# One layer-one planner step: the turn of an output behind more products, and new start times for the threads of the last two head pairs

## The chip, the cores and the metric

The kernel runs on one core of a Trainium2 chip. What counts is the time of one execution on the device, in microseconds (us). Times inside an execution are read from a hardware profile and count from the start of its span.

## What is computed

A trunk of two layers on 1024 tokens of width 1024: a gated linear recurrence (HGRN2) with 16 heads of 128, then forgetting attention (FoX). The change lies in the first layer:

```python
q, fz, i, g = jnp.split(h @ w_in, 4, axis=-1)
logf = jnp.log(lb + (1.0 - lb) * jax.nn.sigmoid(fz))
k = (1.0 - lb) * jax.nn.sigmoid(-fz)
b = jnp.cumsum(logf, axis=3)                       # in chunks of 64 tokens
q_dec, k_in, k_st = q * jnp.exp(b), k * jnp.exp(-b), k * jnp.exp(b_last - b)
att = jnp.where(causal, jnp.einsum('bhnck,bhnsk->bhncs', q_dec, k_in), 0.0)
o_intra = jnp.einsum('bhncs,bhnsv->bhncv', att, v)
...
    o = jnp.einsum('bhck,bhkv->bhcv', qd, state)
    state = dl[..., None] * state + jnp.einsum('bhck,bhcv->bhkv', ks, vv)
...
o = _rms(o, onorm_g.reshape(A_HEADS, HEAD_DIM)).reshape(bsz, s, WIDTH)
return (o * jax.nn.silu(g)) @ w_out
```

## The kernel before

**Two kinds of work.** Layer one multiplies h with 32 weight matrices of 256 columns: for each of eight head pairs p one for v, f, q and g. From the second half of the list on, each is done in seven *steps* (`sa_step`, lines 733 to 760) by a Strassen-like scheme, a step being 12 *products* (matmuls of 128 x 512). A step's weights are made ready two steps ahead (`sa_prep`): GpSimd forms sums (lines 727 to 731), ScalarE rounds (line 242), GpSimd or VectorE subtracts (line 243). The finished columns go to DRAM (lines 644, 647, 758, 759). Beside that VectorE sums modulation weights for later (`mod_sum`, lines 280 and 283, one line 280 and seven lines 283 for each of 24 matrices).

The recurrence of a pair is done by four *threads* (p, i), i = 0 to 3: head j = i % 2, token half th = i // 2. Here they are counted 0 to 31 over all pairs. A thread (`hg_thread`) does:

- *load* (line 494): forget rows f, then q and v, from DRAM into the blocks of its head;
- *forget* (`hg_forget`, lines 495 to 525): ScalarE's sigmoids (502, 503) and logarithm (506), VectorE's scan (507), small steps (513 to 517), ScalarE's exponentials (518 to 521), VectorE's products (522 to 525), GpSimd's line 508;
- *attention* (`hg_att`): 16 small matmuls, the mask (538), four transposes of the keys; *values* (`hg_values`): four transposes;
- *state* (`hg_state`) and *output* (`hg_out`): matmuls, ScalarE's square (580), VectorE's sum (582), the root in twelve small steps (`rsqrt_mean`, lines 231 to 237), and the scaling (584);
- *turn* (`hg_turn`): four transposes of line 584's result on TensorE, ScalarE's line 596, GpSimd's 597, four stores (599).

The blocks of a head are used again by the thread two places on: its load waits for the store of the turn, since f lands where the turn's result lies. Line numbers of matmuls and transposes are those of the recording helpers (48 and 51).

**What sets the order.** The class `Weave` records TensorE's instructions in the order in which they are to run. Products are written out in a plain loop, and each tells the planner by `tick` how much planned time went by; threads are generators that `yield` the planned time until their next part, and a part is put in as soon as it is due. `wait` holds a thread until a mark is set. The recorded order of TensorE is binding. The order of the other engines is made by a scheduler from dependencies and from the program's order, so it moves with TensorE's. `hg_spawn` gives the four threads of a pair their planned start times. Each engine takes its instructions in order; SyncE issues all transfers.

After the list of matrices the output projection of layer one begins (`out_proj`); its first products still alternate with the last threads, 28 to 31.

Of the kernel before, what the change touches and what calls it, by code (L numbers as in the profile page):

```python
# [20 lines left out]
NP = H // 2  # L21
# [72 lines left out]
def hybrid_trunk_kernel(ctx: ExitStack, tc: tile.TileContext, x, c, mod_w, mod_b, norm_g, a_w_in,  # L94
# [4 lines left out]
    PE = Weave(tc, nc.tensor)  # L99
# [391 lines left out]
    def hg_load(p, i):  # L491
        u = us[i % 2]
        for kind, n in (("f", "lf"), ("q", "qd"), ("v", "v")):
            dma(u[n], hgd[kind, p, i])

    def hg_forget(p, i, before):


        j = i % 2
        h, u = 2 * p + j, us[j]  # L500
        oc, lc = oml[:, h:h + 1], lb[:, h:h + 1]
        S.activation(u["k"], u["lf"], AF.Sigmoid, scale=-1.0)
        S.activation(u["lf"], u["lf"], AF.Sigmoid)
        if before is not None:
            S.activation(us[before]["ks"], us[before]["g"], AF.Sigmoid)
        S.activation(u["lf"], u["lf"], AF.Ln, bias=lc, scale=oc)
        V.tensor_tensor_scan(u["b"], rst, u["lf"], 0.0, ALU.mult, ALU.add)  # L507
        G.tensor_scalar(u["k"], u["k"], oc, 0.0, ALU.mult, ALU.add)
        b, k, lf, ks, kst = [ab(u[n]) for n in ("b", "k", "lf", "ks", "kst")]

        dl = sml.tile([P, 8], F32, tag=f"dl{j}", name="dl")
        col = dl.rearrange("p (n o) -> p n o", o=1)
        V.tensor_copy(col[:, 0:4], b[:, :, 0, 63:64])
        V.tensor_copy(col[:, 7:8], b[:, 3:4, 1, 63:64])
        V.tensor_tensor(col[:, 4:7], b[:, 0:3, 1, 63:64], b[:, 1:4, 0, 63:64], ALU.add)
        V.tensor_tensor(lf[:, :, 1, :], spread(dl[:, 4:8], 4, 64), b[:, :, 1, :], ALU.subtract)  # L516
        V.tensor_tensor(b[:, :, 0, :], b[:, :, 0, :], spread(dl[:, 0:4], 4, 64), ALU.subtract)
        S.activation(dl, dl, AF.Exp)
        S.activation(u["ks"], u["b"], AF.Exp, scale=-1.0)
        S.activation(u["eb"], u["b"], AF.Exp)  # L520
        S.activation(lf[:, :, 1, :], lf[:, :, 1, :], AF.Exp)  # L521
        V.tensor_tensor(u["qd"], u["qd"], u["eb"], ALU.mult)  # L522
        V.tensor_tensor(u["ks"], u["ks"], u["k"], ALU.mult)
        V.tensor_tensor(kst[:, :, 1, :], k[:, :, 1, :], lf[:, :, 1, :], ALU.mult)
        V.tensor_tensor(kst[:, :, 0, :], ks[:, :, 0, :], spread(dl[:, 4:8], 4, 64), ALU.mult)
        u["dl"] = dl

    def hg_att(j):

        u = us[j]  # L530
        pa, pk = c128(sm_ps()), sm_ps()
        ks, qd, kst = c128(u["ks"]), c128(u["qd"]), c128(u["kst"])
        for n in range(4):
            PE.matmul(pa[0:64, n, :], lhsT=ks[:, n, 0:64], rhs=qd[:, n, :], start=True, stop=True)
            PE.matmul(pa[64:P, n, 64:P], lhsT=ks[:, n, 64:P], rhs=qd[:, n, 64:P], start=True, stop=True)
        for rows, cs in ((slice(0, 64), slice(0, P)), (slice(64, P), slice(64, P))):
            m = keep[rows, cs]
            V.copy_predicated(u["att"][rows, :, cs],  # L538
                              m.rearrange("p (o q) -> p o q", o=1).broadcast_to([64, 4, m.shape[1]]), pa[rows, :, cs])
        for n in range(4):  # L540
            PE.transpose(pk[:, n * P:(n + 1) * P], kst[:, n, :], ident)
        S.activation(u["kT"], pk, AF.Copy)

    def hg_values(j):

        v, pv = us[j]["v"], sm_ps()
        for n in range(4):
            PE.transpose(pv[:, n * P:(n + 1) * P], v[:, n * P:(n + 1) * P], ident)
        S.activation(v, pv, AF.Copy)

    def hg_state(j, th):

        u = us[j]
        pu = sm_ps()
        kT, st, dl, v = c128(u["kT"]), c128(u["S"]), u["dl"], c128(u["v"])
        nl = 3 if th == 1 else 4
        for n in range(nl):
            PE.matmul(pu[:, n * P:(n + 1) * P], lhsT=kT[:, n, :], rhs=v[:, n, :], start=True, stop=True)
        with tc.high_priority():
            if th == 1:  # L560
                V.tensor_scalar(st[:, 0, :], st[:, 0, :], dl[:, 0:1], None, ALU.mult)
            for n in range(nl):
                if th == 0 and n == 0:
                    V.tensor_copy(st[:, 1, :], pu[:, 0:P])
                else:
                    V.scalar_tensor_tensor(st[:, (n + 1) % 4, :], st[:, n, :], dl[:, 4 + n:5 + n],
                                           pu[:, n * P:(n + 1) * P], ALU.mult, ALU.add)

    def hg_out(j, th):
        u = us[j]  # L570
        po = oa_ps()
        pov = c128(po)
        att, qd, st, v = u["att"], c128(u["qd"]), c128(u["S"]), c128(u["v"])
        for n in range(4):
            first = th == 0 and n == 0
            PE.matmul(pov[:, n, :], lhsT=att[:, n, :], rhs=v[:, n, :], start=True, stop=first)
            if not first:
                PE.matmul(pov[:, n, :], lhsT=qd[:, n, :], rhs=st[:, n, :], start=False, stop=True)
        sq = u["sq"]
        S.activation(sq, po, AF.Square)  # L580
        ss = sml.tile([P, 4], F32, name="ss")
        V.tensor_reduce(ss, c128(sq), AX.X, ALU.add)
        r = rsqrt_mean(ss, 4, 1.0 / P)
        V.tensor_tensor(c128(sq), pov, spread(r, 4, P), ALU.mult)  # L584

    def hg_turn(p, i):

        j, th = i % 2, i // 2
        h, u = 2 * p + j, us[j]
        if (p, i) == (NP - 1, 3):  # L590
            S.activation(u["ks"], u["g"], AF.Sigmoid)
        G.tensor_tensor(u["g"], u["g"], u["ks"], ALU.mult)
        pg = sm_ps()
        for n in range(4):
            PE.transpose(pg[:, n * P:(n + 1) * P], u["sq"][:, n * P:(n + 1) * P], ident)
        S.activation(u["ogT"], pg, AF.Copy, scale=ongc[:, h:h + 1])  # L596
        G.tensor_tensor(u["ogT"], u["ogT"], u["g"], ALU.mult)  # L597
        for n in range(4):
            dma(ogd[th * 4 + n][:, h, :], u["ogT"][:, n * P:(n + 1) * P])

    def hg_thread(p, i):

        j, th = i % 2, i // 2
        first, last = (p, i) == (0, 0), (p, i) == (NP - 1, 3)
        before = (p, i - 1) if i else (p - 1, 3)
        if i >= 2 or p > 0:
            yield from PE.wait(("turn", *((p, i - 2) if i >= 2 else (p - 1, i + 2))))
        for kind in "fqv":
            yield from PE.wait(("mat", kind, p, i))
        hg_load(p, i)  # L610
        yield 3.5
        if not first:
            yield from PE.wait(("gate", *before))
        hg_forget(p, i, None if first else 1 - j)
        PE.marks.add(("forget", p, i))
        yield 9.5
        hg_att(j)
        yield 2.5
        hg_values(j)
        yield from PE.wait(("mat", "g", p, i))  # L620
        dma(us[j]["g"], hgd["g", p, i])
        PE.marks.add(("gate", p, i))
        yield 2.0
        hg_state(j, th)
        yield 4.0
        hg_out(j, th)
        yield 9.0 if p < NP - 2 else 8.0
        if not last:
            yield from PE.wait(("forget", *((p, i + 1) if i < 3 else (p + 1, 0))))
        hg_turn(p, i)  # L630
        PE.marks.add(("turn", p, i))
        yield 0.0
# [65 lines left out]

    def hg_spawn(p):
        for i in range(4):  # L700
            PE.spawn(hg_thread(p, i), {NP - 2: (2.0, 19.0, 35.0, 51.0), NP - 1: (2.0, 14.0, 34.0, 46.0)}.get(
                p, (2.0, 21.0, 40.0, 59.0))[i])


# [59 lines left out]
    G.memset(rst, 1.0)  # L764
    G.memset(c64(rst)[:, :, 0:1], 0.0)
    hg_spawn(0)
    sa_prep(0)
    sa_prep(1)
# [4 lines left out]
    for i, (n, m) in enumerate(SSTEPS):  # L773
        if m == 3 and n + 2 < len(MATS):
            load(a_w(*MATS[n + 2]), 12 + n % 2)
        if m == 7 and n < len(mods_left):
            acc = accs[n % 2]
            mod_sum((18, acc))
            PE.spawn(mod_later(mods_left[n], acc), 8.0)
        if m == 4 and n + 1 < len(mods_left):  # L780
            load(mod_src(mods_left[n + 1]), 18)
        sa_prep(i + 2)
        sa_step(i)
        if m == 4 and MATS[n][0] == "q":
            hg_spawn(MATS[n][1])
# [739 lines left out]
```

## Time and profile before

| | |
|---|---|
| median of three runs | 2527.96 us (2522.85 to 2529.18) |
| the profiled execution | 2524.89 us, its span 2522.9 us |
| TensorE matmuls | 2251.0 us (89%) |
| TensorE weight loads, beside them | 1955.8 us (78%) |
| VectorE | 1717.2 us (68%) |
| ScalarE | 1117.5 us (44%) |
| GpSimd | 879.0 us (35%) |
| mean granted TensorE clock | 0.954 |

The engines are shown as PE (TensorE matmul), PEld (its weight loads), DVE (VectorE), ACT (ScalarE), POOL (GpSimd) and SP (SyncE). A timeline row is a run of like instructions: start, length, engine, line, operation, output and inputs, count, and in brackets the idle time before it with what ended it. The threads of the recurrence run from about 140 to 1170 us of the span.

### The profile page before, as it was taken

The numbers are of one execution on the slowest core, as the hardware profiler recorded it, in microseconds if no ns is written. First come the engines' busy times: TensorE is split into PE (matmuls) and PEld (weight loads), VectorE is DVE, ScalarE is ACT, GpSimd is POOL, SyncE is SP. The second block draws the span as 40 slices with busy tenths as digits, with TensorE's granted clock in tenths as the row PEclk, the third lists the DMA queues.
The fourth block names the chain that finished last, engine by engine and source line by source line (L and its number), as shares of the span: only waits on it lengthen the run. The fifth ranks groups of instructions, "written<-read, shape, count | busy, mean of one in ns | idle before, by whom it ended". The sixth has DMA issues, their size and how long they took to land.

```text
span 2522.9 us, 37602 instructions
## 1 busy us (share of the span) xinstructions
PE 2251.0 (89%) x13384; PEld 1955.8 (78%) x13384; DVE 1717.2 (68%) x4032; ACT 1117.5 (44%) x1850; POOL 879.0 (35%) x755
## 2 busy tenths in 40 slices
PE   4988877887777788889988899989999999999999
PEld 3766666666666677668878899989999999998887
DVE  7687777766676766675586864866777667767633
ACT  5434444444444455563333332444445444455421
POOL 3544444444444455410022222233333333332100
PEclk9999989988888999889999999999999999999999
DMA  7354434344443333474643232351222222325443
GB/s 242 114 163 138 146 119 136 122 137 130 134 137 122 126 113 118 127 246 141 188 137 96 78 118 84 101 167 59 72 78 85 80 86 61 94 74 159 162 144 117
DMA packets 257183, 312.28 MB, mean 124 GB/s; under 512 B 18706, under 2 KB 187060, under 8 KB 256996
## 3 DMA queue, kind: packets, MB, share of 16 engines
q1 hardware_dynamic: 256996, 309.88, 39.0%
q8 instruction: 106, 1.74, 0.3%
q14 instruction: 81, 0.66, 0.1%
HBM read 229.91 MB, written 79.90 MB: 123 GB/s over the span
## 4 chain that ended last, share of the span: by engine, by line
PE 59%; DVE 23%; issue 5%; ACT 3%; DMA 3%; POOL 1%; SPq 0%; DVEq 0%; ACTq 0%; POOLq 0%
PE mm L48 37%; PE oa L48 9%; PE sm L48 7%; PE sm L51 6%; DVE rows4k L283 4%; DVE blk L243 2%; DVE blk L507 1%; DVE rs_t L235 1%; ACT L521 1%; DVE rs_t L232 1%; DVE rs_t L236 1%; DVE rs_y L237 1%; DVE blk L584 1%; DVE blk L758 1%; DVE blk L522 1%
## 5 line engine op out<-in xcount | busy, mean ns | idle before, releaser
L48 PE MATMUL mm<-blk,blk 128*128 128x512 f32 (+1 forms) x7680 | 1615.1, 361 | 59.8 <-DVE blk L243 17.1
L48 PEld LDWEIGHTS mm<-blk,blk 128*128 128x128 f32 x7680 | 1259.6, 195 | 252.9 <-ACT blk L242 32.5
L242 ACT ACTIVATE blk<-blk 128x512 fp32r<-128x512 f32 (+3 forms) x525 | 407.1, 789 | 539.0 <-PE mm L48 334.0
L243 DVE TENSOR_TENSOR blk<-blk,blk 128x1024 fp32r<-128x1024 f32 (+3 forms) x334 | 331.2, 999 | 223.5 <-ACT blk L242 221.6
L243 POOL TENSOR_TENSOR blk<-blk,blk 128x512 fp32r<-128x512 f32 (+1 forms) x191 | 305.6, 1607 | 362.7 <-ACT blk L242 343.1
L48 PE MATMUL oa<-blk,blk 128*128 128x256 f32 (+2 forms) x2364 | 371.7, 302 | 4.0 <-ACT blk L1083 2.8
L51 PE MATMUL sm<-ident,blk 128*128 128x128 f32 x1281 | 208.9, 288 | 165.1 <-DVE blk L584 128.7
L48 PEld LDWEIGHTS oa<-blk,blk 128*128 128x128 f32 x2364 | 326.8, 193 | 26.2 <-ACT blk L1083 3.0
L51 PEld LDWEIGHTS sm<-ident,blk 128*128 128x128 f32 x1281 | 158.7, 147 | 202.6 <-issue 171.7
L48 PE MATMUL sm<-blk,blk 128*128 128x256 f32 (+6 forms) x1800 | 279.2, 315 | 9.8 <-DVE blk L522 7.5
L48 PEld LDWEIGHTS sm<-blk,blk 128*128 128x128 f32 (+2 forms) x1800 | 226.1, 183 | 44.5 <-issue 23.6
L1369 ACT ACTIVATE blk<-blk,m 128x128 f32<-128x128 f32 (+7 forms) x128 | 99.0, 773 | 127.9 <-DVE m L1367 117.5
L283 DVE SCALAR_TENSOR_TENSOR rows4k<-blk,cc,rows4k 128x256 f32<-128x256 f32 x196 | 146.9, 752 | 1.5
L1371 POOL TENSOR_SCALAR blk<-blk,smx 128x128 f32<-128x128 f32 (+7 forms) x128 | 97.7, 764 | 135.6 <-DVE smx L1370 118.2
L1341 POOL TENSOR_TENSOR blk<-rows4k,keep 128x128 f32<-128x128 f32 x128 | 62.7, 490 | 227.3 <-DVE mx L1348 208.5
L243 DVE TENSOR_TENSOR blk<-sm,blk 128x512 fp32r<-128x512 f32 (+1 forms) x160 | 93.0, 581 | 62.9 <-ACT blk L242 62.3
L538 DVE COPY_PREDICATED blk<-keep,sm 64x512 f32<-64x512 int32 x64 | 38.0, 593 | 115.6 <-PE sm L48 115.1
L242 ACT ACTIVATE blk<-sm 128x512 fp32r<-128x512 f32 (+1 forms) x160 | 81.1, 507 | 48.9 <-PE sm L51 48.1
L1348 DVE CUSTOM_DVE_ANT_0 blk<-sm,rows4k 128x128 f32<-128x128 f32 (+3 forms) x176 | 84.7, 495 | 23.0 <-PE sm L48 21.0
L521 ACT ACT_TABLE_LOAD x30 | 38.5, 1283 | 110.6 <-DVE blk L516 86.2
L597 POOL TENSOR_TENSOR blk<-blk,blk 128x512 f32<-128x512 f32 x32 | 43.0, 1344 | 107.2 <-ACT blk L596 107.1
L596 ACT ACTIVATE blk<-sm,cc 128x512 f32<-128x512 f32 x32 | 22.0, 688 | 131.2 <-PE sm L51 131.2
(185 smaller groups left out, 2203.3 us busy)
## 6 DMA issues: line engine op xcount, KB each, us to landing
blk<-in_a_w_in_dram SPq DMA_DIRECT2D x64, 512.0 KB, 4.5
blk<-in_mod_w_dram SPq DMA_DIRECT2D x48, 512.0 KB, 3.9
blk<-in_kv_w_dram SPq DMA_DIRECT2D x32, 512.0 KB, 3.9
blk<-in_b_w_in_dram SPq DMA_DIRECT2D x32, 512.0 KB, 3.9
blk<-hf SPq DMA_DIRECT2D x32, 256.0 KB, 2.8
blk<-hq SPq DMA_DIRECT2D x32, 256.0 KB, 3.8
blk<-hv SPq DMA_DIRECT2D x32, 256.0 KB, 2.7
blk<-hg SPq DMA_DIRECT2D x32, 256.0 KB, 2.9
```

The source lines that it names most:

```text
L48: self._chain(self.PE.matmul(*a, **k))
L51: self._chain(self.PE.transpose(*a, **k))
L242: S.activation(hi, src, AF.Copy)
L243: eng.tensor_tensor(lo, src, hi.bitcast(F32), ALU.subtract)
L283: V.scalar_tensor_tensor(acc, rawk(rb, k), csil[:, k:k + 1], acc, ALU.mult, ALU.add)
L521: S.activation(lf[:, :, 1, :], lf[:, :, 1, :], AF.Exp)
L538: V.copy_predicated(u["att"][rows, :, cs], m.rearrange("p (o q) -> p o q", o=1).broadcast_to([64, 4, m.shape[1]]), pa[rows, :, cs])
L597: G.tensor_tensor(u["ogT"], u["ogT"], u["g"], ALU.mult)
L1341: G.tensor_tensor(nfm, nF[:, i * P:n], negm, ALU.add)
L1348: V.tensor_tensor_reduce(dst, src, add, 1.0, -3e38, ALU.add, ALU.max, mx[:, nm:nm + 1])
L1369: S.activation(l[:, 0:n], l[:, 0:n], AF.Exp, bias=m, accum_out=sm)
L1371: G.tensor_scalar(l[:, 0:n], l[:, 0:n], sm, 0.0, ALU.mult, ALU.add)
```

## The change

Three numbers of the planner change: the planned time from a thread's output to its turn, 9.0 (8.0 in the last two pairs) to 13.5 (10.0), and start times of threads in the last two pairs.

```diff
         hg_out(j, th)
-        yield 9.0 if p < NP - 2 else 8.0
+        yield 13.5 if p < NP - 2 else 10.0
         if not last:
...
-            PE.spawn(hg_thread(p, i), {NP - 2: (2.0, 19.0, 35.0, 51.0), NP - 1: (2.0, 14.0, 34.0, 46.0)}.get(
+            PE.spawn(hg_thread(p, i), {NP - 2: (2.0, 21.0, 38.0, 54.0), NP - 1: (2.0, 13.0, 34.0, 46.0)}.get(
```

What that does to the order is seen in a middle thread. On TensorE before, at thread 17's attention (sm from blk_0_819 and blk_1_818), the turn of thread 16 (transposes of blk_1_814) stands six products ahead of it:

```order
L48 MATMUL mm<-blk_0_825,blk_0_1033 128x512
L51 MATMUL sm<-ident,blk_1_814 128x128 x4
L48 MATMUL mm<-blk_0_81,blk_0_1031 128x512
L48 MATMUL mm<-blk_1_82,blk_0_1031 128x512
L48 MATMUL mm<-blk_0_81,blk_0_1031 128x512 x2
L48 MATMUL mm<-blk_1_82,blk_0_1031 128x512
L48 MATMUL mm<-blk_0_81,blk_0_1031 128x512
L48 MATMUL sm<-blk_0_819,blk_1_818 64x128
L48 MATMUL sm<-blk_0_819,blk_1_818 64x64
```

On TensorE now, the same turn stands behind that attention, its key transposes, 12 products, the transposes of the values (blk_1_820) and three products:

```order
L51 MATMUL sm<-ident,blk_1_820 128x128 x4
L48 MATMUL oa<-blk_0_91,blk_1_1032 128x512
L48 MATMUL oa<-blk_1_92,blk_1_1032 128x512
L48 MATMUL oa<-blk_0_91,blk_1_1032 128x512
L51 MATMUL sm<-ident,blk_1_814 128x128 x4
L48 MATMUL oa<-blk_0_91,blk_1_1032 128x512
L48 MATMUL oa<-blk_1_92,blk_1_1032 128x512
```

So the turn moved past six products, the attention and 15 more products; the distances between the attentions stay 81, 84 and 87 products up to the last pairs.

On VectorE before, behind the state (line 566) of thread 17, the scan of thread 18 comes first, with the sums of the modulation weights (280, 283) in and behind its forget chain; the sum of thread 17's output (582) stands behind the whole chain:

```order
L507 SCALAR_TENSOR_TENSOR blk_1_814<-blk_1_822,blk_0_813 128x512
L289 TENSOR_REDUCE cc<-sm 128x2
L513 COPY dl<-blk_1_814 128x4
L514 COPY dl<-blk_1_814 128x1
L290 TENSOR_TENSOR cc<-cc 128x2
L515 TENSOR_TENSOR dl<-blk_1_814 128x3
L280 TENSOR_SCALAR rows4k<-blk_0_105,cc 128x256
L516 TENSOR_TENSOR blk_0_813<-dl,blk_1_814 128x4x64
L517 TENSOR_TENSOR blk_1_814<-blk_1_814,dl 128x4x64
L283 SCALAR_TENSOR_TENSOR rows4k<-blk_0_105,cc,rows4k 128x256
```

On VectorE now, at the same place, all seven of line 283 and line 582 come first, and the scan stands among the steps of the root:

```order
L283 SCALAR_TENSOR_TENSOR rows4k<-blk_0_105,cc,rows4k 128x256 x3
L283 SCALAR_TENSOR_TENSOR rows4k<-blk_1_106,cc,rows4k 128x256 x4
L758 TENSOR_TENSOR blk_1_822<-mm,blk_0_115 128x512
L582 TENSOR_REDUCE ss<-blk_1_818 128x4
L231 TENSOR_SCALAR rs_m<-ss 128x4
L232 TENSOR_SCALAR rs_t<-rs_m 128x4
L233 TENSOR_SCALAR rs_y<-rs_t 128x4
L235 SCALAR_TENSOR_TENSOR rs_t<-rs_y 128x4
L236 TENSOR_TENSOR rs_t<-rs_t,rs_m 128x4
L237 SCALAR_TENSOR_TENSOR rs_y<-rs_t,rs_y 128x4
L235 SCALAR_TENSOR_TENSOR rs_t<-rs_y 128x4
L507 SCALAR_TENSOR_TENSOR blk_1_814<-blk_1_822,blk_0_813 128x512
```

What moved: the sums went ahead of the scan, and line 584 (the root's end) from behind the forget chain to the middle of it.

## Rows read from the trace of the kernel before

**Rows 1.** Stretches: length, PE, PEld, DVE, ACT, POOL busy (count), clock, DMA share, GB/s.
```profile
686.00:822.50 136.50, 108.04 (x546) 86.25 (x545) 96.53 (x190) 61.17 (x97) 61.89 (x49) 0.90 0.42 131
1480.00:2523.00 1043.00, 1026.69 (x6915) 944.40 (x6914) 661.36 (x1985) 443.80 (x835) 300.80 (x336) 1.00 0.33 102
```
**Rows 2.** Waits from 686 to 822.5: engine, line, waited for, us, times, longest.
```profile
PE sm L51 <- DVE blk L584: 23.1, 4, 6.9
```
**Rows 3.** Timeline of TensorE in the middle of the stage.
```profile
693.66 1.72 PE L48 MATMUL oa<-blk,blk 128*128 128x128 f32 x14
...
702.54 3.17 PE L48 MATMUL mm<-blk,blk 128*128 128x512 f32 x12 [1.01 <-DVE rs_m L231]
712.65 1.09 PE L51 MATMUL sm<-ident,blk 128*128 128x128 f32 x4 [6.94 <-DVE blk L584]
713.39 2.85 PE L48 MATMUL mm<-blk,blk 128*128 128x512 f32 x6
716.17 1.09 PE L48 MATMUL sm<-blk,blk 128*64 128x128 f32 x16
...
745.37 1.08 PE L51 MATMUL sm<-ident,blk 128*128 128x128 f32 x4 [5.67 <-DVE blk L584]
...
748.95 1.67 PE L48 MATMUL sm<-blk,blk 128*64 128x128 f32 x16
```
**Rows 4.** Stretches behind a turn's wait, columns as in rows 1.
```profile
712.65:716.20 3.55, 3.55 (x12) 2.57 (x12) 0.00 (x0) 1.97 (x2) 1.28 (x1) 0.52 0.02 5
717.20:735.00 17.80, 17.80 (x95) 15.15 (x95) 13.80 (x26) 11.67 (x19) 8.75 (x7) 1.00 0.41 129
```
**Rows 5.** Timelines of SyncE, ScalarE and VectorE, the load and chains between two turns.
```profile
719.04 0.32 SPq L494 DMA_DIRECT2D blk<-hf  x1
...
722.88 0.61 ACT L502 ACTIVATE blk<-blk 128x512 f32<-128x512 f32 x1
...
726.32 1.23 DVE L507 TENSOR_TENSOR_SCAN blk<-blk,blk 128x512 f32<-128x512 f32 x1 [0.81 <-ACT blk L506]
...
734.21 0.42 DVE L525 TENSOR_TENSOR blk<-blk,dl 128x256 f32<-128x256 f32 x1
...
744.53 0.69 DVE L584 TENSOR_TENSOR blk<-oa,rs_y 128x512 f32<-128x512 f32 x1
```
**Rows 6.** The chain that ended last, one piece behind the stage: start, us, what.
```profile
1168.25 67.35 PE mm L48 x297
```
**Rows 7.** Timelines of TensorE and VectorE: turns, attentions that waited, a long chain's ends.
```profile
678.06 0.69 PE L51 MATMUL sm<-ident,blk 128*128 128x128 f32 x4 [2.75 <-DVE blk L584]
...
708.89 0.41 DVE L525 TENSOR_TENSOR blk<-blk,dl 128x256 f32<-128x256 f32 x1
...
969.77 0.63 PE L51 MATMUL sm<-ident,blk 128*128 128x128 f32 x4 [2.53 <-DVE blk L584]
...
992.01 1.06 PE L48 MATMUL sm<-blk,blk 128*64 128x128 f32 x16 [0.64 <-DVE blk L522]
...
1095.58 0.60 PE L51 MATMUL sm<-ident,blk 128*128 128x128 f32 x4
...
1119.57 1.94 PE L48 MATMUL sm<-blk,blk 128*64 128x128 f32 x16 [4.04 <-DVE blk L522]
```
**Rows 8.** Timeline of TensorE: attentions of threads 0, 5, 22 and 28.
```profile
143.79 1.09 PE L48 MATMUL sm<-blk,blk 128*64 128x128 f32 x16
...
306.53 1.09 PE L48 MATMUL sm<-blk,blk 128*64 128x128 f32 x16
...
885.46 1.68 PE L48 MATMUL sm<-blk,blk 128*64 128x128 f32 x16
...
1068.35 1.09 PE L48 MATMUL sm<-blk,blk 128*64 128x128 f32 x16
```
**Rows 9.** Timelines of GpSimd and VectorE at one moment.
```profile
727.37 1.28 POOL L243 TENSOR_TENSOR blk<-blk,blk 128x512 fp32r<-128x512 f32 x1 [0.96 <-ACT blk L242]
...
727.77 0.90 DVE L513 COPY dl<-blk 128x4 f32<-128x4 f32 x1
```

## The prediction

> **What bounds the kernel now.** I first read the table by stretches [rows 1]. Through the middle of layer one TensorE is busy 108 us of 136.5 in each group of four threads, at a mean granted clock of 0.90; VectorE has 97, ScalarE and GpSimd 62 each. No engine is full, so a chain of waits sets the pace there. After that stage (out of the change's reach) TensorE is nearly full. The waits [rows 2] name the gap: four times in a group, 23.1 us together, TensorE stands before the four transposes of a *turn* and waits for line 584, VectorE's last step of the thread's output. TensorE's own timeline [rows 3] shows it: the output matmuls of a thread at 693.66, the products that stand before the turn, 6.94 us of nothing, the turn at 712.65, six products, the next thread's attention at 716.17; then the same again with 5.67 us. The clock follows the gap [rows 4]: behind it 0.52, the lower of its two levels (1.2 of 2.4 GHz), for some 3.5 us, then 1.00. So one turn costs its wait and about 2 us of slow matmuls.
>
> Why is line 584 late? [rows 5] follow one thread. The turn of 712.65 lets SyncE load the forget rows of the thread after next (issue 719.04); ScalarE starts on them at 722.88, the scan of line 507 runs at 726.32, the forget chain ends with line 525 at 734.63. Only then does VectorE finish the reduction and the root of the thread in between: line 584 at 744.53, and the turn of 745.37 waits for it. From turn to turn that is a **loop** of 32.7 us: about 22 us of load and forget chain, about 10.6 us of output chain. The attention of the next thread does not need the output chain at all; it needs the forget chain, which was ready at 734.6, and its matmuls stood in line behind the turn until 748.95.
>
> **The change part by part.** No instruction is added or removed; only the order moves (front part, two pieces of the order).
>
> *The turn goes behind the next attention.* For nearly all threads the four transposes now stand 15 products behind that attention and 60 products behind the output matmuls, where there were 39. From output to turn there are now 60 products at 0.227 us (67.35 us for 297 of them [rows 6]), 13.6 us, and the attention. Before, the turn that line 584 releases came 19.0 us after the start of the output matmuls (693.66 to 712.65); now output, products, attention and transposes alone are some 18 us of TensorE, its new wait comes on top, and in the new order of VectorE line 584 stands ahead of the end of the forget chain, not behind it. So the wait on line 584, 5.8 us a thread, goes, with the slow matmuls behind it.
>
> *What is late next: the attention itself.* The loop now runs: attention of thread i, 15 products, turn of thread i-1, store, load for thread i+1, forget chain, attention of thread i+1. Its two terms:
> (a) From attention to turn. At full clock: 1.09 for the attention [rows 3], 0.63 each for two groups of transposes [rows 7], 15 x 0.227 = 3.4, together 5.7 us. Behind a gap, with the slow clock: 1.94 as behind the 4.04 us wait at 1119.57 [rows 7], 1.09 for transposes as at 712.65, six products at 0.46 (2.78 us for six at 713.39 [rows 3]), nine at 0.227, one group of transposes 0.6: 8.4 us. I take 6.8, nearer neither end, since a gap remains but a smaller one.
> (b) From the turn to the attention that needs its load. Where the attention of before did wait for its forget chain, the chain can be read whole [rows 7]: turn 969.77 to attention 992.01, 22.2 us; turn 1095.58 to attention 1119.57, 24.0 us. The thread of [rows 5] gives 22.0 from the turn to the end of line 525. The longest in the middle of the stage runs from the turn at 678.06 to line 525 at 708.89 + 0.41: 31.2 us. What makes the long one long is in the order: sums of the modulation weights (line 283) and the load behind other issues stand in it. In the new order seven of line 283 stand together ahead of line 582, so ahead of the scan, while VectorE waits for the load anyway; but some steps of the root and two further steps now stand inside the forget chain, and on ScalarE two or three further copies. I take 23.4, near the short rows. Ends for the range: 22.0 and 31.2.
> Period 6.8 + 23.4 = **30.2 us a thread**. TensorE's own need is 84 x 0.227 = 19.1 and some 5.7 for the thread's other matmuls, 24.8; VectorE's is 96.5 / 4 = 24.1 [rows 1]. Both lie below, so the loop sets the end, and TensorE waits about 3 to 4 us before each attention.
>
> *SyncE's queue.* The stores of a turn come later against the other issues, so a weight load and one or two stores of products now stand ahead of them, and one store or one load between them and the forget load. Each issue takes 0.32 us [rows 5], and the products they wait for lie ahead of the turn in TensorE's order. Cost nil beside the turn; if one of them were late, its delay would enter (b).
>
> *The sum*, by the start times of the attentions [rows 8]:
> - threads 5 to 22: 885.46 - 306.53 = 578.9 us for 17 gaps, 34.05 each. At 30.2: 513.4, a gain of 65.5.
> - threads 0 to 5: 162.7 us. The first attention waits for no turn, the gap of thread 3 to 4 has only 75 products, and the turn of thread 3 goes 24 products behind attention 4. I take 30.2 where the loop closes and 28 to 32 elsewhere: 157, a gain of 6.
> - threads 22 to 28: 1068.35 - 885.46 = 182.9 us. The new starts of the last threads give gaps of 84, 87, 84, 75, 69 and 108 products (before 84, 87, 75, 69, 72, 120). By loop or by products, the larger: 29.8, 29.8, 29.0, 22.7, 27.7, 31.6, together 170.6, a gain of 12. What goes are waits before turns like that of 2.53 us [rows 7].
> - behind thread 28 the order of TensorE is the same but for nine products at one turn: nothing.
> Gain 83.5 us. The profiled execution took 2524.89 us, its span 2522.9; the median of the runs is 2527.96, 3 us more. 2524.9 - 83.5 = 2441.4; I say **2441**.
>
> **A rule against it.** At 727.77 VectorE's copy of four columns took 0.90 us and ended at 728.67; GpSimd's operation of 727.37 ended at 728.65 [rows 9]. The short step stood until the long one on the other engine was over. In the new order GpSimd has line 508, three of line 243 and line 728 beside the forget chain, five where the chain of [rows 5] met about three. If each of the two more stops one step of the chain for a whole operation of 1.28 us, the period is 30.2 + 2.6 = 32.8. The Trainium skill ("SBUF — State Buffer", Who interferes with whom) says it as a rule: VectorE with two SBUF inputs and GpSimd share a port pair that is locked for a whole instruction, and the loser stands still. By that rule the trace agrees.
>
> **The rivals.**
> 1. *The gap becomes too short for the clock to fall.* Then (a) is 5.7 and (b) may be 22.2: 27.9 us a thread, gains 105, 9 and 16: 2395. For it: behind the 2.53 us wait at 969.77 the transposes took 0.63, not 1.09 [rows 7]. Against: TensorE would still wait 3 us.
> 2. *More small steps stopped by GpSimd*: 32.8 a thread, gains 21, 4 and 10: 2490.
> 3. *The load chain stays as it was*, a mean of short and long ones near 27: 33.8 a thread, the wait only changes its name, from turn to attention: 2520, no change that can be seen. For it: of the two chains read in the middle one is 31.2, and their mean is 26.6. Against: the sums that stretched the long one stand elsewhere now.
> 4. *Slower: the later turn feeds a slow load.* The load can't start before the turn's store has left, and the turn is about 10 us later against the attention than it was. If the chain is 31.2 in every thread, the period is 38.0, the middle loses 67 and the start 10: 2600. It decides from a chain of 34.05 - 6.8 = 27.3 us on. Against: of the four chains read three are 24.0 or shorter.
> That the change does not do what it says is excluded by the order.
>
> **How the numbers follow.** Forecast 0.60, rival 1 0.17, rival 2 0.08, rival 3 0.09, rival 4 0.06. Faster by over 0.3% (about what a measurement of this kernel can tell): 0.60 + 0.17 + 0.08 = 0.85; within 0.3%: 0.09; slower: 0.06. The range runs from rival 1 to rival 2, 2395 to 2490, and holds 0.85.
>
> **What would show it.** Right: no wait of a turn on line 584 in the middle; instead attention matmuls (line 48, 128 x 64) waiting on line 522 for 2 to 5 us; attentions 29 to 32 us apart; turn to next-but-one attention 22 to 25 us; VectorE's busy share in the middle up to some 80%. Rival 1 shows gaps near 28 and a clock near 1.00; rival 2 shows small VectorE steps of over 1 us between lines 507 and 522; rivals 3 and 4 show ScalarE's line 502 waiting for the load late, or gaps of 34 and more. It would be wrong at its root if TensorE waited elsewhere, for a prepared weight (line 243), longer than before each attention.

## The result and the profile after

The changed kernel took **2501.49 us** (median of 4 runs, 2500.13 to 2504.52), the kernel before 2527.11 beside it: a ratio of 0.9902 (95% interval 0.9885 to 0.992). It is faster, by some 25 us where 86 were forecast, and lies above the range. The profiled span is 2499.5 us, 23.4 less than before.

The waits moved as forecast. Two groups of the page of the changed kernel (operation, output, inputs, count, busy and mean; then the idle time ahead and what ended it) show that line 584 no longer ends most of what the turn's transposes wait (128.7 us of 165.1 in the kernel before), and that the attention waits for line 522 instead; from 300 to 890 us no wait on line 584 is left:

```profile
L48 PE MATMUL sm<-blk,blk 128*128 128x256 f32 (+6 forms) x1800 | 289.2, 325 | 129.1 <-DVE blk L522 129.0
L51 PE MATMUL sm<-ident,blk 128*128 128x128 f32 x1281 | 208.1, 287 | 45.5 <-DVE blk L1074 12.0
```

The table by stretches, for four threads in the middle (columns as in [rows 1]), and the waits of that stretch (as in [rows 2]):

```profile
700.34:830.43 130.09, 105.70 (x544) 86.62 (x545) 98.11 (x189) 61.27 (x96) 61.68 (x49) 0.92 0.44 138
```
```profile
PE sm L48 <- DVE blk L522: 19.0, 4, 6.4
```

Where 23.1 us of waiting stood before four turns, 19.0 stand before four attentions. Four threads take 130.1 us and not 136.5. TensorE's timeline gives the attentions of threads 0, 5, 22 and 28 (the counterpart of [rows 8]):

```profile
142.97 1.09 PE L48 MATMUL sm<-blk,blk 128*64 128x128 f32 x16
...
307.52 1.75 PE L48 MATMUL sm<-blk,blk 128*64 128x128 f32 x15 [9.54 <-DVE blk L522]
...
865.10 1.06 PE L48 MATMUL sm<-blk,blk 128*64 128x128 f32 x16 [2.66 <-DVE blk L522]
...
1052.89 1.09 PE L48 MATMUL sm<-blk,blk 128*64 128x128 f32 x16
```

The differences of these times, in us, with those of before and of the forecast:

| Stretch | Before | Forecast | After |
|---|---|---|---|
| threads 0 to 5 | 162.7 | 157 | 164.6 |
| threads 5 to 22 (17 gaps) | 578.9 | 513.4 | 557.6 |
| threads 22 to 28 | 182.9 | 170.6 | 187.8 |
| thread 28 to the end of the span | 1454.6 | 1454.6 | 1446.6 |

So the gap in the middle is 557.6 / 17 = **32.8 us**, where 30.2 were forecast and 34.05 stood before. 44 of the 60 us that are missing lie there. (In this table they come to 61, since the first attention came 0.8 us earlier.)

One turn of the loop can be read whole. TensorE, from an attention to its turn and to the next attention:

```profile
733.28 1.10 PE L48 MATMUL sm<-blk,blk 128*64 128x128 f32 x16 [4.22 <-DVE blk L522]
734.31 1.12 PE L51 MATMUL sm<-ident,blk 128*128 128x128 f32 x4
735.08 2.78 PE L48 MATMUL mm<-blk,blk 128*128 128x512 f32 x6
...
740.22 0.60 PE L51 MATMUL sm<-ident,blk 128*128 128x128 f32 x4
...
766.38 1.06 PE L48 MATMUL sm<-blk,blk 128*64 128x128 f32 x16 [2.73 <-DVE blk L522]
```

Term (a), attention to turn, is 740.22 - 733.28 = 6.9 us: forecast 6.8. Term (b), turn to the attention that needs its load, is 26.2: forecast 23.4. As means of the 17 gaps of threads 5 to 22 they are 6.8 and 26.0, so all that the gap is too long lies in (b). The timelines of SyncE, ScalarE, VectorE and GpSimd say where it grew:

```profile
746.06 0.32 SPq L494 DMA_DIRECT2D blk<-hf  x1
...
748.83 0.63 ACT L502 ACTIVATE blk<-blk 128x512 f32<-128x512 f32 x1 [2.91 <-DMA blk<-hf]
...
751.93 0.82 ACT L506 ACTIVATE blk<-blk,cc 128x512 f32<-128x512 f32 x1
...
745.55 1.41 DVE L280 TENSOR_SCALAR rows4k<-blk,cc 128x256 f32<-128x256 f32 x1
...
747.00 5.80 DVE L283 SCALAR_TENSOR_TENSOR rows4k<-blk,cc,rows4k 128x256 f32<-128x256 f32 x7
752.71 0.68 DVE L758 TENSOR_TENSOR blk<-mm,blk 128x512 f32<-128x512 f32 x1
753.31 0.68 DVE L582 TENSOR_REDUCE ss<-blk 128x4 f32<-128x512 f32 x1
754.02 1.16 DVE L231 TENSOR_SCALAR rs_m<-ss 128x4 f32<-128x4 f32 x1
...
756.29 1.22 DVE L507 TENSOR_TENSOR_SCAN blk<-blk,blk 128x512 f32<-128x512 f32 x1
...
763.17 1.40 DVE L525 TENSOR_TENSOR blk<-blk,dl 128x256 f32<-128x256 f32 x1
764.49 1.75 DVE L522 TENSOR_TENSOR blk<-blk,blk 128x512 f32<-128x512 f32 x1
...
763.01 2.68 POOL L243 TENSOR_TENSOR blk<-blk,blk 128x512 fp32r<-128x512 f32 x2 [7.85 <-ACT blk L242]
```

Set beside the chain of [rows 5] (turn 712.65), piece by piece: turn to load issue 5.8 us (before 6.4); to line 502 2.8 (3.8); to the start of the scan 7.5 (3.4); from there to the end of the chain 9.95 (8.3). Only two pieces grew. **The scan comes 4 us later**: ScalarE's line 506, whose result it takes, ends at 752.75, but VectorE reaches the scan only at 756.29, 3.5 us behind it (3.5 as a mean of the 17 gaps, 0.2 before). The sums (280, seven of 283) take VectorE up to 752.71, and lines 758 and 582 and seven steps of the root follow them. The other 0.5 us is ScalarE's: line 580 now stands ahead of line 506. **The end of the chain is 1.6 us longer**: GpSimd's two operations of line 243 run from 763.01 to 765.69, and lines 525 and 522 beside them take 1.40 and 1.75 us.

### The profile page after: what moved, and what is told of

It reads as the page before. It is cut to its first block, busy times and chain, and to the rows that moved or that the text cites. A ratio compares the mean times of both kernels' runs of the same rounds, so it can differ in the third digit from the quotient of the medians.

```text
span 2499.5 us, 37703 instructions
## 1 busy us (share of the span) xinstructions
PE 2240.1 (90%) x13384; PEld 1960.7 (78%) x13384; DVE 1717.3 (69%) x4032; ACT 1115.1 (45%) x1850; POOL 880.6 (35%) x755
## 4 chain that ended last, share of the span: by engine, by line
PE 57%; DVE 19%; DMA 6%; issue 6%; ACT 4%; POOL 2%; SPq 1%; DVEq 0%; ACTq 0%; POOLq 0%
PE mm L48 35%; PE oa L48 9%; PE sm L48 8%; PE sm L51 6%; DVE rows4k L283 4%; DVE blk L243 2%; DVE blk L522 2%; DMA blk<-hf 1%; ACT blk L242 1%; DVE rows4k L280 1%; DVE blk L523 1%; ACT L521 1%; DMA blk<-in_a_w_out_dram 1%; DVE blk L507 1%; DVE rs_t L235 1%
## 5 line engine op out<-in xcount | busy, mean ns | idle before, releaser
L48 PE MATMUL mm<-blk,blk 128*128 128x512 f32 (+1 forms) x7680 | 1588.7, 358 | 50.3 <-DVE blk L243 29.7
L243 DVE TENSOR_TENSOR blk<-blk,blk 128x1024 fp32r<-128x1024 f32 (+3 forms) x334 | 348.3, 1049 | 223.7 <-ACT blk L242 221.9
L48 PE MATMUL sm<-blk,blk 128*128 128x256 f32 (+6 forms) x1800 | 289.2, 325 | 129.1 <-DVE blk L522 129.0
L48 PE MATMUL oa<-blk,blk 128*128 128x256 f32 (+2 forms) x2364 | 381.7, 305 | 3.8 <-ACT blk L1083 2.6
L48 PEld LDWEIGHTS sm<-blk,blk 128*128 128x128 f32 (+2 forms) x1800 | 234.2, 189 | 160.1 <-issue 124.8
L597 POOL TENSOR_TENSOR blk<-blk,blk 128x512 f32<-128x512 f32 x32 | 42.7, 1335 | 67.6 <-ACT blk L596 64.9
L592 POOL TENSOR_TENSOR blk<-blk,blk 128x512 f32<-128x512 f32 x32 | 42.1, 1315 | 54.2 <-ACT blk L505 54.2
```

The source lines that it names most:

```text
L48: self._chain(self.PE.matmul(*a, **k))
L243: eng.tensor_tensor(lo, src, hi.bitcast(F32), ALU.subtract)
```

## The experiments

The theory after this reading, S in the expectations: the sums of the modulation weights, which the change put ahead of the scan, set term (b). Its rivals: the loop would be this long without them (the load chain itself, or GpSimd's stops). Ratios are against the kernel before of the same batch, with 95% intervals.

**The two parts of the change apart.** One kernel has the yields of the change with the old starts of the last pairs, the other the new starts with the old yields.

```
only_yield:   {NP - 2: (2.0, 19.0, 35.0, 51.0), NP - 1: (2.0, 14.0, 34.0, 46.0)}
only_starts:  yield 9.0 if p < NP - 2 else 8.0
```

> The planned time to the turn of the changed kernel with the start times of before. Both theories: the middle as in the changed kernel (gaps of 33), gain of the middle 17 to 20 us; the last pairs decide what the table of start times is worth: 2498 to 2510.

> The start times of the changed kernel in the last two pairs with the old planned time to the turn. Theory S and any other: the middle as before (gaps of 34); what the table is worth without the later turn lies in threads 22 to 31 alone: 2515 to 2530.

Measured: 2506.92 us, 0.9924 (0.9907 to 0.994), and 2526.19, 0.9983 (0.9972 to 0.9995), both within what was expected. The gaps of threads 5 to 22 are those of the changed kernel in the first (32.7) and those of before in the second (34.1). The yields carry most of the gain, the starts a few us, and the 44 us that are missing in the middle belong to the yields.

**The sums cut short**, in the changed kernel and in the kernel before. The kernel leaves out six of the seven steps of line 283 in each sum; line 280 and one step stay.

```diff
-    def mod_sum(*todo):
+    def mod_sum(*todo, steps=range(1, KT)):
...
-        for k in range(1, KT):
+        for k in steps:
...
-            mod_sum((18, acc))
+            mod_sum((18, acc), steps=(4,))
```

> The changed kernel with two steps instead of eight in each sum of modulation weights (line 280 and one line 283 of seven; the sums are thus wrong, the matmuls and transfers stay). Theory S (the scan, line 507, waits for VectorE, which is still at the sums and the root steps behind them): 4.5 us less of VectorE ahead of the scan, so the scan starts within 0.2 us of line 506's end, the middle gaps between attentions fall from 33 to 29.5 to 30, the total to 2435 to 2455. Theory L (the gap is the time from attention to turn plus load and forget chain, whatever VectorE does): gaps stay 32 to 33, 2490 to 2502. Theory P (steps behind the scan are stopped by GpSimd's operations, some 2 us a thread): gaps stay 32 to 33 as well.

> The kernel before with the same sums cut to two steps of eight. In it the sums stand in the forget chain or among the root steps, both on the loop from turn to turn of 34 us. Theory S: it falls too, to gaps of 30 to 32 and 2465 to 2495, since the sums lie in the loop here as well; the change without sums is then worth some 30 to 50 us. Theory L (in the changed order the sums cost nothing, in the old one they do): it falls by more than the changed kernel does.

Measured: 2452.21 us, 0.9707 (0.969 to 0.9724), and 2458.24, 0.9732 (0.9716 to 0.9748). In the changed kernel with the sums cut short the scan follows line 506 at once (0.2 us behind its end as a mean), here at 741.35 where 506 ends at 741.01 (ScalarE's and VectorE's timelines):

```profile
740.19 0.82 ACT L506 ACTIVATE blk<-blk,cc 128x512 f32<-128x512 f32 x1
...
734.97 1.46 DVE L283 SCALAR_TENSOR_TENSOR rows4k<-blk,cc,rows4k 128x256 f32<-128x256 f32 x1
...
738.40 0.69 DVE L582 TENSOR_REDUCE ss<-blk 128x4 f32<-128x512 f32 x1
...
741.35 1.22 DVE L507 TENSOR_TENSOR_SCAN blk<-blk,blk 128x512 f32<-128x512 f32 x1
...
749.13 1.75 DVE L522 TENSOR_TENSOR blk<-blk,blk 128x512 f32<-128x512 f32 x1
```

The gaps of threads 5 to 22 are 30.4 us: near the 30.2 of the forecast, and 2.4 less than with whole sums. Of the 3.3 us by which the scan comes earlier behind line 506, 1.0 is lost again between it and the attention. S holds. Line 522 is still stopped here (1.75 us), so the gaps can come down to the forecast with that stop in place. The second run has the surprise, and its expectation was wrong by half: the kernel *before* gains even more from the shorter sums, some 68 us where the changed kernel gains some 49 (gaps 30.8, expected 30 to 32, but a time of 2458 for the 2465 and more expected). That is the sign that theory L named, but not L: in the changed order the sums do cost something. With the sums cut short the change is worth some 6 us, not tens, and single runs of the two kernels overlap. So some 19 of the changed kernel's 25 us come from the sums costing less at their new place. In either order they stood in the loop: before, in and behind the forget chain and so ahead of line 584; after, ahead of the scan. The change passed them from one client to the other.

**A turn earlier by 2.5 units of planned time**, which also puts the scan ahead of the root's steps in VectorE's order, with the sums still ahead of both.

```diff
-        yield 13.5 if p < NP - 2 else 10.0
+        yield 11.0 if p < NP - 2 else 10.0
```

> The changed kernel with 11.0 in place of 13.5: the turn stands three products behind the next attention instead of 15, so its load starts some 3.4 us earlier; in VectorE's order the scan then stands directly behind the sums, ahead of the root steps. Theory S: the early load buys nothing by itself, line 507 starts 3 us or more behind the end of line 506, at the moment the sums end; what is won is the root steps ahead of the scan, 2 to 3 us a gap: gaps 30 to 31, 2445 to 2465. Theory L: line 507 follows line 506 directly and the gaps fall by 3.4 us to 29.6, 2440. Theory P: gaps fall by 3.4 minus nothing, as L.

Measured: 2459.11 us, 0.9732 (0.9714 to 0.975); gaps 31.1. The time is as expected, the gaps just above. The scan still starts 3.5 us behind the end of line 506 as a mean (2.0 to 4.5), now behind the sums themselves, which take longer here (line 283 1015 ns for 770). From attention to turn 3.0 us are won, from the turn to line 502 2.9 are lost again; what is left is a shorter way from the scan to the attention (8.6 us for 9.5), where neither line 522 (682 ns) nor 525 (412) is stopped, and 0.7 us on ScalarE. So the time came out as theory S said, but the run does not show that the root's steps gave it. It does show that the changed kernel's own constant isn't the best one of its kind.

**The sums at another place** ("late" in the labels), in the changed kernel, in the kernel before, and with earlier turns (yield 11.0 and 12.0). The program emits them two steps of a matrix earlier; in VectorE's order they then stand behind a forget chain, around the mask of its attention, and end some 12 us before the next scan's input is ready.

```diff
-        if m == 7 and n < len(mods_left):
+        if m == 2 and n < len(mods_left):
...
-            PE.spawn(mod_later(mods_left[n], acc), 8.0)
+            PE.spawn(mod_later(mods_left[n], acc), 24.0)
```

> The changed kernel with all its work, but each sum of modulation weights is emitted two products steps of its matrix earlier in the program (at step 2 rather than 7, its columns' transposes correspondingly later), which in VectorE's order puts it behind the forget chain of the next thread, ahead of and around the attention's mask, instead of ahead of the scan. Theory S: as with the sums cut: the scan follows line 506 within a microsecond, gaps of 30 to 31, 2450 to 2465. Were it VectorE's total work and not its place that holds the kernel, gaps stay near 32.5 and the total near 2495.

> The kernel before with the sums moved the same way. In its loop from turn to turn the sums stood among forget chain or root steps; behind line 584 they cost less. Theory S: gaps fall from 34 to about 31, as with the sums cut, 2460 to 2480; then the change and the sums' place are two ways to the same gap, and the change adds little on top. If the turn's place is what matters, gaps stay at 33 to 34 and 2510 or more.

> 11.0 in place of 13.5 (the turn three products behind the attention) and the sums moved late. Theory S: with the sums away from the scan the load is what the scan waits for, so now the earlier turn pays: gaps fall below those of the late sums with 13.5 by up to 3 us, to 27.5 to 29.5, 2400 to 2440. If VectorE's or TensorE's own work were the floor already, gaps stay at 30 to 31, 2450.

> Late sums with 12.0 in place of 13.5: the turn stands nine products behind the attention instead of 15, nothing else in the order of VectorE moves much. With the scan now waiting for the load, the loop is attention to turn plus chain: six products at 0.23 to 0.46 us less, gaps fall by 1.4 to 2 us from 29.7 to about 28, 2410 to 2425. If the loop is not what holds the late-sums kernel any more, 2440 to 2450.

Measured: in the changed kernel 2445.45 us, 0.9676 (0.966 to 0.9692), gaps 29.75, both a little better than expected; in the kernel before 2565.3, 1.0145 (1.0125 to 1.0166), slower where a gain was expected; with yield 11.0 2481.87, 0.9815 (0.9799 to 0.9831); with yield 12.0 2465.82, 0.9759 (0.974 to 0.9778). The other three expectations missed, all to the slow side. The first shows that the place counts and not the work: all of it is done, and the scan follows line 506 at once (0.03 us). From the scan to the attention it takes 7.6 us for 9.5, since line 522 isn't stopped either (683 ns), but the load comes later: 2.0 us of the gain are lost between the turn and the end of line 506. SyncE's queue in the kernel before with late sums, with GpSimd's line 597 (the turn's product that the store sends) and ScalarE's first step on the load, shows one reason:

```profile
663.07 1.48 POOL L597 TENSOR_TENSOR blk<-blk,blk 128x512 f32<-128x512 f32 x1
...
664.58 1.74 SPq L599 DMA_DIRECT2D ogd<-blk  x4
666.42 4.34 SPq L250 DMA_DIRECT2D blk<-in_mod_w_dram  x2
671.82 0.34 SPq L759 DMA_DIRECT2D hq<-rows4k  x1
672.34 0.34 SPq L494 DMA_DIRECT2D blk<-hf  x1
...
677.95 0.63 ACT L502 ACTIVATE blk<-blk 128x512 f32<-128x512 f32 x1 [9.26 <-DMA blk<-hf]
```

The store left at 664.58, right behind line 597, but two loads of weights for the sums (4.34 us for the two issues) and the store of line 759 now stand ahead of the forget load, which is issued 7.8 us behind the end of line 597 (3.2 at the turn of [rows 5]) and lands late: line 502 waits 9.26 us for it. The gaps are 33 to 41 us. With yield 11.0 the turn itself also waits, for a reduction of the sums (TensorE's waits, 470 to 800):

```profile
PE sm L48 <- DVE blk L522: 26.5, 8, 6.3
PE sm L51 <- DVE cc L289: 9.3, 5, 3.4
```

And there the weight loads stand ahead of the store itself (GpSimd, then SyncE):

```profile
718.37 1.29 POOL L597 TENSOR_TENSOR blk<-blk,blk 128x512 f32<-128x512 f32 x1 [3.05 <-ACT blk L596]
...
718.24 5.17 SPq L250 DMA_DIRECT2D blk<-in_mod_w_dram  x2
723.50 1.96 SPq L599 DMA_DIRECT2D ogd<-blk  x4
```

Line 597 ended at 719.66, its store goes at 723.50. So the sums can't be moved freely: their loads sit in the queue of the loop's own load. No run moved the loads alone, so their share of the cost is not shown. With yield 12.0 the turn comes 2.1 us earlier behind the attention, as meant (means of the 17 gaps, against late sums with 13.5), but the way from the turn to line 502 is 1.7 us longer and that from the scan to the attention 1.2, where line 522 takes 1165 ns for 683.

**One subtraction of the prepared weights moved from GpSimd to VectorE**, in the changed kernel as it stands and with late sums.

```diff
-        halves(V if m in (6, 5) else G, *sa_slot(i), ...
+        halves(V if m in (6, 5, 4) else G, *sa_slot(i), ...
```

> The changed kernel with one subtraction of the prepared weights (line 243, step 4 of a thread) taken from GpSimd to VectorE, the sums left where the change put them. Theory of two causes: beside the sums ahead of the scan, GpSimd's two operations of line 243 stop the last steps of the forget chain (line 522 takes 1750 ns as a mean in the middle of the stage against 689 before, line 525 takes 952 against 415, together 1.6 us a thread). If that stop lies on the path, and one of the two operations carries it, line 522 falls to 700 to 1100 ns, the gap of threads 5 to 22 falls from 32.8 to 31.3 to 32.0 us, and the time from 2501 to 2470 to 2488 us. Rival: the sums alone set the loop; what the shorter step gives is lost again since VectorE has the subtraction in addition, 2495 to 2510 us, gaps 32.5 to 33.

> Late sums with one of GpSimd's subtractions of a matrix (line 243 of step 4) given to VectorE, so that it can't run against VectorE's last steps of the forget chain. Theory P: line 525 or 522, of which one takes 1.5 us or more beside GpSimd's line 243, falls to its 0.4 or 0.7; VectorE gets 0.7 us more: gaps fall by 0 to 0.5 us, 2435 to 2448. If those steps are not stopped by GpSimd, their length stays, and gaps rise by 0.7 us to 30.4: 2455 to 2462.

Measured: 2460.61 us, 0.9727 (0.9711 to 0.9744), and **2423.74 us, 0.9586 (0.9568 to 0.9604), the fastest of all**, 4.1% below the kernel before. Both beat their expectations. The end of the forget chain in the first (VectorE, then GpSimd):

```profile
762.80 0.68 DVE L522 TENSOR_TENSOR blk<-blk,blk 128x512 f32<-128x512 f32 x1
763.40 1.49 DVE L525 TENSOR_TENSOR blk<-blk,dl 128x256 f32<-128x256 f32 x1
...
763.28 1.32 POOL L243 TENSOR_TENSOR blk<-blk,blk 128x512 fp32r<-128x512 f32 x1 [8.95 <-ACT blk L242]
```

One operation of GpSimd is left where two stood, and it stops line 525, which now comes behind line 522; the attention waits for 522. The groups by shape from 470 to 800 us (columns as in the page's groups), of the kernel before, the changed kernel and this one, in that order:

```profile
L513 DVE COPY dl<-blk 128x4 f32<-128x4 f32 x10 | 10.6, 1059 | 0.0
L522 DVE TENSOR_TENSOR blk<-blk,blk 128x512 f32<-128x512 f32 x9 | 6.2, 689 | 0.0
L525 DVE TENSOR_TENSOR blk<-blk,dl 128x256 f32<-128x256 f32 x9 | 3.7, 415 | 0.0
```
```profile
L522 DVE TENSOR_TENSOR blk<-blk,blk 128x512 f32<-128x512 f32 x11 | 19.2, 1750 | 0.0
L525 DVE TENSOR_TENSOR blk<-blk,dl 128x256 f32<-128x256 f32 x11 | 10.5, 952 | 0.4
L513 DVE COPY dl<-blk 128x4 f32<-128x4 f32 x10 | 1.7, 166 | 0.0
```
```profile
L525 DVE TENSOR_TENSOR blk<-blk,dl 128x256 f32<-128x256 f32 x11 | 16.4, 1491 | 0.0
L522 DVE TENSOR_TENSOR blk<-blk,blk 128x512 f32<-128x512 f32 x11 | 7.5, 683 | 0.0
L513 DVE COPY dl<-blk 128x4 f32<-128x4 f32 x11 | 1.8, 165 | 0.0
```

On the path to the attention that is 0.95 + 1.75 = 2.7 us in the changed kernel against 0.68 here, 2.0 less; the gaps of threads 5 to 22 fell from 32.8 to 30.9, 1.9 less. The scan is as late as it was (3.6 us behind line 506 as a mean); the way from it to the attention went from 9.5 to 7.7. Whether the fewer operations or the exchanged order of 525 and 522 gives it was not taken apart: both came together. With late sums the order is 522 ahead of 525 already, and there the same edit takes the gaps from 29.75 to 28.8, with 6.6 us from the scan's start to the attention where there were 7.6. The step that the expectation named did not give it: line 525 keeps its 1.49 us. It is line 237, a step of the root that stands behind the scan, three in each thread (groups from 470 to 800, without and with the edit):

```profile
L237 DVE SCALAR_TENSOR_TENSOR rs_y<-rs_t,rs_y 128x4 f32<-128x4 f32 x34 | 18.2, 534 | 0.8
L237 DVE SCALAR_TENSOR_TENSOR rs_y<-rs_t,rs_y 128x4 f32<-128x4 f32 x33 | 7.6, 230 | 0.8
```

Behind the scan GpSimd had two operations of line 243 in a row, which stopped one line 236 and one line 237; one is left, and line 237 runs free, 0.9 us a thread.

## Why the forecast was wrong

**The start of the argument was right.** The wait on line 584 goes from the middle, the attention waits for line 522 in its place, four times in four threads, and term (a) is 6.8 us as forecast. Of the sign that would have made it wrong at its root, longer waits for a prepared weight, little is seen: from 300 to 890 us products wait 24.2 us for line 243, attentions 89.0 for line 522.

**The step that failed is term (b), 23.4 us, measured 26.0 as a mean (26.2 in the turn shown)**, and in it one sentence: "In the new order seven of line 283 stand together ahead of line 582, so ahead of the scan, while VectorE waits for the load anyway". The wait is there, but the sums use up all of it: they run from 745.55 to 752.71, and the load has gone through ScalarE by 752.75 (as a mean the sums end 0.3 us before it). Lines 758 and 582 and seven steps of the root, which stand behind them and ahead of the scan, therefore run when the scan could, and it starts at 756.29. The sum has nothing for these 3.5 us. The order had shown these rows in a line; I did not add up their durations against the time that the load leaves. Cutting the sums short gives 30.4 us a thread, with 6.7 for (a) and 23.8 for (b); 2.4 x 17 = 41 of the 44 us that the middle fell short.

**The stop by GpSimd** was weighed as a rival at +2.6 us. It is real, and moved: line 513 lost 0.9 us of it (1059 ns to 166), line 522 got 1.06 and line 525 0.54. By these three lines that is 0.7 us more than in the chain of before, and 1.9 us a thread could be had back (2460.61). The rule cited in the prediction (the Trainium skill, "SBUF — State Buffer", Who interferes with whom) fits lines 522 and 525, which have two inputs: they stand beside GpSimd's operations and end 0.3 to 0.6 us behind them, less than the 0.42 and 0.69 us that they take alone. The copy of line 513, from which the prediction read that the trace agrees, has one input and is no case of the rule as it was put there. The rival's period, 32.8, is the measured one by luck: it took 2.6 us for more stops and nothing for the late scan. Taken away singly, the sums give back 2.4 us and the stop 1.9, of 2.6 in all; no run took both away, so how they share the distance is not shown. Its 2490 misses by what the ends did.

**The ends.** Threads 0 to 5 gained nothing (164.6 for 157 forecast; the loop is the same). Threads 22 to 28 lost 4.9 us where 12 should have been gained. Of these 17 us, 5.8 lie in the gap of threads 25 to 26 (28.5 for 22.7) and 10.6 in that of 27 to 28, taken as 108 products in 31.6 us. It is 42.2, mainly since the turn in it still waits for line 584. TensorE's timeline, the turn in the kernel before and then the changed kernel:

```profile
1055.99 1.08 PE L51 MATMUL sm<-ident,blk 128*128 128x128 f32 x4 [6.61 <-DVE blk L584]
```
```profile
1010.65 1.94 PE L48 MATMUL sm<-blk,blk 128*64 128x128 f32 x16 [5.87 <-DVE blk L522]
...
1044.39 1.08 PE L51 MATMUL sm<-ident,blk 128*128 128x128 f32 x4 [8.69 <-DVE blk L584]
1045.12 7.84 PE L48 MATMUL mm<-blk,blk 128*128 128x512 f32 x27
1052.89 1.09 PE L48 MATMUL sm<-blk,blk 128*64 128x128 f32 x16
```

That turn was not among those that went behind an attention, and its wait of 6.61 us should have been carried over. The sums are not behind it: the gap is 41.9 with the sums cut short. No run took it apart further. Behind thread 28 the step "nothing" was wrong the other way: 8 us were gained. They need both parts of the change: with the yields alone that stretch takes 1454.9 us, with the starts alone 1456.2. Why is not shown.

**The other rivals.** The clock stayed up in some turns only: behind the wait of 4.22 us the six products of 735.08 took 2.78 us, 0.46 each, at a granted clock of 0.54, near the lower of the two levels; behind that of 2.73 us it was 1.00. In four of the 17 gaps (a) is 5.4 us, near rival 1's 5.7, in the others 6.8 to 8.2. The load chain did not stay as it was: it lost 1.6 us up to line 502. Rival 3's 27 us for (b) are near the 26.0 measured all the same, for another reason, the late scan. Slower did not come; its mechanism, a slow load in the loop, was met in the kernel before with late sums (1.0145), and from another cause, the issues ahead of it on SyncE.

**The range** failed for another reason than the value. Its upper end is rival 2's and has the measured period, 32.8, which is luck; what put the time above it is the ends, where it counted 14 us of gain and about 2 came.

## What to carry to other kernels

When a wait is taken away, sum up what every in-order engine has queued ahead of the *next* waited-for step, in us, against the time at which its input is there: work that looks like filler costs from the moment when it and what stands behind it, up to that step, take longer than the wait (here 10.7 us against 7.2). Work that no one waits for is still in the loop of whoever stands behind it; an order that hands it from one chain to another gains only the difference between the two places (some 19 of the 25 us here). And moving it drags its loads along, in a queue that the loop's own load shares: try such a move in the order in which it will run, since the same edit gave 2.2% in one order and cost 1.4% in the other.

## What the runs showed of the hardware

Two of GpSimd's 128 x 512 operations in a row stopped two steps of VectorE in a row (952 and 1750 ns for 415 and 689, as means), and one operation stopped one (1491 for 415). What that costs depends on which of the steps stands on the path: where line 525 alone is stopped, behind line 522, TensorE waits 0.8 us in all for it from 470 to 800 us; with both stopped the gaps are 1.9 us a thread longer. Of TensorE's clock: behind waits of 2.66 and 2.73 us the attention took 1.06 us at a granted clock of 1.00, as with no wait (1.09); behind 4.22 us it took 1.10 at 0.92, but the six products behind it 2.78 at 0.54; behind 5.87 us it took 1.94 at 0.50. In the kernel before an attention behind 2.79 us (at 1022.53) took 1.27 at 0.80, so the length of the wait alone did not decide.
